# Token sums in sixteen steps among the weight parts, the next layer's memory norm inside the output product, and tanh for a reciprocal: a two-layer hybrid block on one core

## The chip, the cores and the metric

One core of a Trainium2 chip runs the whole kernel: two layers of a hybrid block for 1024 tokens of width 1024. Its engines are TensorE (PE), VectorE (DVE), ScalarE (ACT), GpSimd (POOL) and SyncE (SP); SP issues every DMA of this kernel, in order. The metric is the time of one execution on the device in microseconds, as the median of several runs.

## What is computed

Each layer normalizes the tokens, computes four branches (a gated MLP that mixes tokens in chunks, a sparse attention, an attention with a forget gate, an attention over a memory of 256 rows), multiplies each by a gate, adds them up, and projects the sum back onto the residual:

```python
def hybrid_layer(x, mem, ...):
    h = rms_norm(x, g_pre)
    parts = jnp.split(h @ w_in, IN_SPLITS, axis=-1)
    y_a = chunked_gmlp(a_u, a_v, ...) * jax.nn.silu(a_z)
    y_b = nsa_attention(b_q, ..., b_g, ...) * jax.nn.silu(b_z)
    y_c = forgetting_attention(c_q, c_k, c_v, c_f, c_fbias) * jax.nn.silu(c_z)
    y_m = memory_attention(m_q, mem, g_mem, w_mem_kv) * jax.nn.silu(m_z)
    ys = jnp.stack([y_a, y_b, y_c, y_m], axis=2)
    up = jnp.einsum('bsnw,nwd->bsnd', ys, w_br)
    gates = jax.nn.sigmoid(jnp.einsum('bsd,dne->bsne', h, w_gate))
    merged = jnp.einsum('bsnd,bsnd->bsd', gates, up)
    return x + rms_norm(merged @ w_o, g_post)
```

In `forgetting_attention` the gate enters as `log_sigmoid(f_logit + f_bias)`, summed over the tokens. In `memory_attention` the keys and values are `rms_norm(mem, g_mem) @ w_mem_kv`.

## The kernel before, in words

Every float32 matmul is done as three matmuls on operands split into a high and a low part. ACT copies the high part (L330) and DVE or POOL subtracts it from the operand to get the low one (`split`, L332). A block of weights is loaded by one DMA of 512 KB into one of two `wr` buffers, ACT copies `wh` (L227) and POOL subtracts `wl` (L229); for the names that begin with mk, mv, av and cv POOL does the first 512 columns and DVE the rest (L231).

A layer runs in this order. **The front** normalizes the memory rows and projects keys and values from them (`mem_kv`), then normalizes eight tiles of 128 tokens (`prenorm`); both transpose each tile on TensorE (L395). **The gates** follow. `proj_wide` (L300) multiplies a token half by a wide weight in four parts, 24 matmuls each; it runs for `av` on each half (each result goes through a GELU of two ACT and two DVE operations, L348 to L351, into `gv`) and for `cv` on each half. Between these products stands `token_sums`, a generator that prepares sums and differences of token quarters for a product with fewer multiplications (`quarter_mm`, L471). For each of four quarters POOL does four additions (L431), four operations on them (L432 to L435) and four split subtractions (L332: `t2l`, `t1l`, `t3l`, `t4l`), while ACT makes `t1h` to `t4h` after the last GELU. Nine `gate_pair`s of seven such products follow. Inside the first runs `forget`, the chain for the forget gate: ACT Abs (L561) and Exp (L564), DVE sums (L566, L567) and a reciprocal (L569), ACT `Ln` (L570), which needs another table in ACT, so a load of 1.28 us stands ahead of it and one behind. **The attention** stage computes the branches' heads; its outputs go to DRAM (`o`), are read back (`oo`, L1199), multiplied by a gate `z` (L340, L341, L1201) and stored (`y`, L1202). **The merge** reads a branch's `y` back as eight `yf` tiles (L1301), splits them into `yh` and `yl`, multiplies them by `u` weights (L251, L254, L255 on `yh`), and adds them up with gates `th` that are loaded (L1310) or computed. `out_proj` then multiplies the sum `mhh`, `mhl` by `w_o` for each token half (384 matmuls each), and the next layer's front begins.

The kernel is written in program order. A scheduler gives each engine and SP's DMA queue its own order, decided by the times that it reckons with. It also keeps the buffers of a pool in turn: the first write of a tile waits for the first write of the tile that stood before it in the same pool. `gate_out(1, "bz", 3)` is the last gate of the sparse attention: it reads what the last head stored and, in the kernel before, is called within branch 0 of the merge.

Of the kernel before, what the change touches and what calls it, by code (L numbers as in the profile page):

```python
# [19 lines left out]
F32 = mybir.dt.float32  # L20
# [193 lines left out]
class Net:  # L214
# [71 lines left out]

    def proj_wide(self, name, hi, lo, done, tail=False):


        v = "p (k c) -> p k c"  # L290
        ps = [self.pj() for _ in range(4)]
        for parts in ((0,), (1,), (2, 3)) if tail else ((0,), (1,), (2,), (3,)):
            w = [(x, [z.rearrange(v, c=512) for z in self.weight(f"{name}_{x}")]) for x in parts]
            for i in range(4):
                ts = slice(i * 128, i * 128 + 128)
                for x, (wh, wl) in w:
                    for k in range(2):
                        kk = 2 * x + k
                        for n, (a, b) in enumerate(((hi, wh), (hi, wl), (lo, wh))):
# [100 lines left out]
    def layer(self, l):  # L400
# [3 lines left out]
        nb = self.bufs  # L404
        with p("kf", 4) as self.pkk, p("vf", 3) as self.pvv, p("tf", 1) as self.ptp:
            self.front()
        with p("pp", nb["pp"]) as self.ppp:
# [9 lines left out]
    def token_sums(self):  # L417
# [8 lines left out]
        for k in range(4):  # L426
# [3 lines left out]
            for x, z in ((x11, b11), (x12, b12), (x22, b22), (x21, b21)):  # L430
                nc.tensor_add(x, f(z[0][:, k]), f(z[1][:, k]))  # L431
            nc.tensor_sub(x1, x12, x11)  # L432
            nc.tensor_sub(x22, x22, x12)
            nc.tensor_add(x11, x11, x22)
            nc.tensor_sub(x21, x21, x11)  # L435
            yield
            with self.tc.issue_after(self.last_act.ins):
                for n, x in (("t2", x11), ("t1", x1), ("t3", x22), ("t4", x21)):
                    self.split(t[n][0][:, k], t[n][1][:, k], x, pool=True)

# [113 lines left out]
    def forget(self):  # L554


        nc, fb, r = self.nc, self.fb[32:40], slice(32, 40)
        f, m, u = ([self.st(n)[r] for _ in range(2)] for n in ("ff", "fm", "fu"))
        x = [z[r] for z in self.fp]
        for c in range(2):  # L560
            nc.scalar.activation(f[c], x[c], AF.Abs, bias=fb)  # L561
            nc.vector.tensor_scalar(m[c], x[c], fb, 0.0, op0=OP.add, op1=OP.min)
        for c in range(2):
            nc.scalar.activation(f[c], f[c], AF.Exp, scale=-1.0)  # L564
        for c in range(2):
            nc.vector.tensor_scalar_add(u[c], f[c], 1.0)  # L566
            nc.vector.scalar_tensor_tensor(f[c], u[c], 1.0, f[c], op0=OP.subtract, op1=OP.subtract)  # L567
        for c in range(2):
            nc.vector.reciprocal(x[c], u[c])  # L569
            nc.scalar.activation(u[c], u[c], AF.Ln)  # L570
            nc.vector.tensor_mul(f[c], f[c], x[c])
# [105 lines left out]

    def fox_values(self, c):
        def done(i, ps):
            for x in range(2):  # L680
                self.value_tile(ps[:, x * 256:x * 256 + 256], c * 4 + i, x * 4)
        self.proj_wide("cv", self.hh[c], self.hl[c], done)

# [370 lines left out]

    def gmlp_v(self, c):

        def done(i, ps):
            t = self.st("gv")
            self.gelu2(t, ps, 512)
            self.nc.sync.dma_start(self.gvd[c * 4 + i], t)  # L1060
        self.proj_wide("av", self.hh[c], self.hl[c], done)

# [38 lines left out]

    def mem_kv(self):

        nc, a, l = self.nc, self.a, self.l
        mt = [[self.pkk.tile([128, 4, 256], R32, name="mt", tag="slot") for _ in range(2)] for _ in range(2)]
# [3 lines left out]
        with self.hot():  # L1109
            self.norm_t(a["mem"], a["g_mem"][l], 2, put)  # L1110
        m = lambda y, k: mt[y][k // 4][:, k % 4, :]
        for h in range(4):
# [104 lines left out]

    def front(self):
# [3 lines left out]
        self.mem_kv()  # L1222
        self.prenorm()
        self.early = True
        if self.l == 0:
            self.load("win", "anyc")

    def gates(self):
        sums = self.token_sums()
        self.turn2 = 0  # L1230
        next(sums)
        self.gmlp_v(0)
        next(sums)
        self.gmlp_w()
        self.gmlp_v(1)
        next(sums)
        self.fox_values(0)
        next(sums)
        self.fox_values(1)
        next(sums, None)  # L1240
        self.gmlp_sums()
# [28 lines left out]
    def merge(self):  # L1270
        nc, tc, a, l = self.nc, self.tc, self.a, self.l
        p = lambda n, b: tc.tile_pool(name=n, bufs=b, reuse_waits="tile")
        with p("acc", 1) as pacc, p("yh", 5) as self.pyh:
            self.acc = [pacc.tile([128, 8, 512], F32, name=f"acc{c}") for c in range(2)]
            for n in (0, 2, 3, 1):
                self.add_branch(n)
            gp = self.pyh.tile([128, 1024], F32, name="gp", tag="yh")
            nc.sync.dma_start(gp, a["g_post"][l].partition_broadcast(128))
            self.early = "banks"
            for c in range(2):  # L1280
                self.out_proj(c, gp)

    def add_branch(self, n):
        yy = [self.get_y(n, c) for c in range(2)]
        for cs in ((0, 1),) if n != 1 else ((0,), (1,)):
            for e in range(8):
                if n == 0 and e == 3:
                    self.gate_out(1, "bz", 3)
                wg = None if (n, e, 0) in self.ready else self.a_form(f"g{n}{e}")
# [158 lines left out]
```

## Time and profile before

| | |
|---|---|
| median of 3 runs (lowest to highest) | 3180.48 us (3177.91 to 3187.18) |
| profiled execution, its time | 3182.38 us |
| its span | 3180.3 us |
| TensorE busy (share) | 3056.4 us (96%) |
| DVE busy | 1876.5 us (59%) |
| ACT busy | 1485.2 us (47%) |
| POOL busy | 1450.7 us (46%) |

A busy share is an average over stages. In a timeline each row is an instruction with its start and duration in us, the engine, the line, the operation with its output and inputs, and in brackets the idle time of the engine before it with what released it. Lines are those of the kernel before.

### The profile page before, as it was taken

The numbers are of one execution on the slowest core, as the hardware profiler recorded it, in microseconds if no ns is written. First come the engines' busy times: TensorE is split into PE (matmuls) and PEld (weight loads), VectorE is DVE, ScalarE is ACT, GpSimd is POOL, SyncE is SP. The second block draws the span as 40 slices with busy tenths as digits, with TensorE's granted clock in tenths as the row PEclk, the third lists the DMA queues.
The fourth block names the chain that finished last, engine by engine and source line by source line (L and its number), as shares of the span: only waits on it lengthen the run. The fifth ranks groups of instructions, "written<-read, shape, count | busy, mean of one in ns | idle before, by whom it ended". The sixth has DMA issues, their size and how long they took to land.

```text
span 3180.3 us, 45150 instructions
## 1 busy us (share of the span) xinstructions
PE 3056.4 (96%) x15168; PEld 2554.8 (80%) x15168; DVE 1876.5 (59%) x4297; ACT 1485.2 (47%) x3309; POOL 1450.7 (46%) x1158
## 2 busy tenths in 40 slices
PE   7899999999999999999988999999999999999998
PEld 6678888887888888788776788788878888887887
DVE  6355447768666855336373554477686678653363
ACT  5333345556556555313353333455565555553232
POOL 6755445443232323258467444454432332332584
PEclk9999999999999999999999999999999999999999
DMA  6444486654334322456563444955542343234564
GB/s 219 127 133 130 149 252 170 181 178 128 101 106 146 110 88 93 149 172 196 187 194 122 136 133 146 256 171 173 186 133 88 112 142 107 87 96 159 175 195 146
DMA packets 251672, 475.15 MB, mean 149 GB/s; under 512 B 42512, under 2 KB 96784, under 8 KB 251440
## 3 DMA queue, kind: packets, MB, share of 16 engines
q1 hardware_dynamic: 251440, 472.26, 47.7%
q8 instruction: 120, 1.97, 0.3%
q14 instruction: 112, 0.92, 0.1%
HBM read 334.73 MB, written 137.43 MB: 148 GB/s over the span
## 4 chain that ended last, share of the span: by engine, by line
PE 81%; DMA 4%; POOL 4%; DVE 4%; issue 3%; ACT 3%; SPq 1%; DVEq 0%; POOLq 0%; ACTq 0%
PE pj L255 11%; PE pj L251 11%; PE pj L254 11%; PE s L471 6%; PE o L633 5%; PE s L300 5%; PE pt L621 5%; PE s L254 4%; PE pj L471 4%; PE s L255 4%; PE s L251 4%; PE pj L300 3%; PE s L589 3%; PE s L590 3%; POOL wl L229 2%
## 5 line engine op out<-in xcount | busy, mean ns | idle before, releaser
L229 POOL TENSOR_TENSOR wl<-wr,wh 128x1024 fp32r<-128x1024 f32 (+1 forms) x232 | 525.2, 2265 | 597.3 <-ACT wh L227 519.2
L255 PE MATMUL pj<-hh,wl 128*128 128x512 f32 x1648 | 652.1, 396 | 2.3 <-POOL wl L229 2.3
L251 PE MATMUL pj<-hh,wh 128*128 128x512 f32 x1648 | 651.2, 395 | 2.5 <-DVE z L341 1.9
L254 PE MATMUL pj<-hl,wh 128*128 128x512 f32 x1648 | 650.2, 395 | 0.0
L227 ACT ACTIVATE wh<-wr 128x1024 fp32r<-128x1024 f32 x232 | 245.7, 1059 | 361.5 <-DMA wr<-wt 90.6
L599 ACT ACTIVATE p<-p,nm 128x384 f32<-128x384 f32 (+3 forms) x512 | 306.8, 601 | 208.7 <-DVE nm L594 204.9
L332 DVE TENSOR_TENSOR pt<-pt,pt 128x512 fp32r<-128x512 f32 (+1 forms) x464 | 292.4, 635 | 145.7 <-ACT pt L330 144.3
L255 PEld LDWEIGHTS pj<-hh,wl 128*128 128x128 f32 x1648 | 310.5, 188 | 62.7 <-POOL wl L229 3.5
L251 PEld LDWEIGHTS pj<-hh,wh 128*128 128x128 f32 x1648 | 310.6, 188 | 60.8 <-DVE z L341 2.8
L330 ACT ACTIVATE pt<-pt 128x512 fp32r<-128x512 f32 (+1 forms) x464 | 252.3, 554 | 224.0 <-PE pt L621 164.6
L254 PEld LDWEIGHTS pj<-hl,wh 128*128 128x128 f32 x1648 | 310.3, 188 | 57.8
L633 PE MATMUL o<-pt,v 128*128 128x512 f32 (+1 forms) x864 | 245.6, 371 | 8.0 <-DVE pt L332 7.9
L642 POOL TENSOR_TENSOR yt<-yt 128x256 f32<-128x256 f32 x128 | 100.0, 781 | 293.8 <-ACT yt L641 234.1
L621 PE MATMUL pt<-ident,p 128*128 128x128 f32 x1488 | 231.3, 272 | 0.3 <-DVE pt L332 0.2
L621 PEld LDWEIGHTS pt<-ident,p 128*128 128x128 f32 x1488 | 185.1, 140 | 42.7 <-DVE pt L332 0.7
L251 PE MATMUL s<-yh,wh 128*128 128x512 f32 x512 | 200.2, 394 | 6.8 <-ACT yh L330 5.3
L589 PE MATMUL s<-kd,q 128*128 128x512 f32 (+2 forms) x512 | 187.5, 369 | 15.6 <-DVE nm L594 15.6
L254 PE MATMUL s<-yl,wh 128*128 128x512 f32 x512 | 200.9, 392 | 1.1 <-DVE yl L334 1.1
L255 PE MATMUL s<-yh,wl 128*128 128x512 f32 x512 | 200.2, 391 | 0.0
L590 PE MATMUL s<-kl,q 128*128 128x512 f32 (+2 forms) x512 | 175.7, 345 | 0.0
L633 PEld LDWEIGHTS o<-pt,v 128*128 128x128 f32 x864 | 147.9, 189 | 32.4 <-DVE pt L332 11.0
L664 DVE TENSOR_SCALAR p<-p,r,sg 128x384 f32<-128x384 f32 (+2 forms) x320 | 167.0, 577 | 1.7
(378 smaller groups left out, 6598.0 us busy)
## 6 DMA issues: line engine op xcount, KB each, us to landing
wr<-wt SPq DMA_DIRECT2D x250, 512.0 KB
th<-thd SPq DMA_DIRECT2D x124, 256.0 KB
thd<-gu SPq DMA_DIRECT2D x72, 256.0 KB
q<-rq SPq DMA_DIRECT2D x32, 512.0 KB
yf<-y SPq DMA_DIRECT2D x64, 256.0 KB
thd<-th SPq DMA_DIRECT2D x52, 256.0 KB
vd<-vs SPq DMA_DIRECT2D x48, 256.0 KB
v<-vd SPq DMA_DIRECT2D x24, 512.0 KB
```

What stands on the lines that cost most here:

```text
L229: nc.gpsimd.tensor_sub(lo[:, :n], raw[:, :n], hi.bitcast(F32)[:, :n])
L251: ins = nc.tensor.matmul(out, ah, bh, start=k == 0, stop=False)
L254: nc.tensor.matmul(out, ah, bl, start=False, stop=False)
L255: nc.tensor.matmul(out, al, bh, start=False, stop=k == n - 1)
L300: self.nc.tensor.matmul(ps[i], a[:, kk, ts], b[:, k], start=kk == n == 0, stop=kk == 7 and n == 2)
L332: (nc.gpsimd if pool else nc.vector).tensor_sub(lo, src, hi.bitcast(F32))
L471: nc.tensor.matmul(out, w[a][:, k], t[b][:, k], start=start and k == x == 0, stop=k == 3 and x == 2, skip_group_check=True)
L589: self.mark(nc.tensor.matmul(ps[:, :w], q[:, tq], kd[:, b0:b0 + w], start=True, stop=False), 1 + n / 128)
L590: nc.tensor.matmul(ps[:, :w], q[:, tq], kl[:, b0:b0 + w], start=False, stop=True)
L599: nc.scalar.activation(p[:, :n], p[:, :n], AF.Exp, bias=init, scale=-1.0, accum_out=l[:, x:x + 1])
L621: nc.tensor.transpose(pt[:, off + x * 128:off + x * 128 + 128], src, self.ident)
L633: nc.tensor.matmul(o[:, :, t0:t0 + m], it["v"], w[:, :, off:off + m], start=first, stop=last)
```

## The change

- `token_sums` yields sixteen times and not five, and `proj_wide` calls it (`among`) at each of its four weight parts, in `av` and `cv` on both halves. Each quarter is cut in four: the additions, the four operations, the splits of t2 and t1, the splits of t3 and t4. The subtractions of t3 and t4 move from POOL to DVE (`pool=False`).
- `mem_norm` is cut off from `mem_kv`. For layer 2 it is called between the two halves of the output product of layer 1, and `fresh`, `mem_kv` and `prenorm` of layer 2 directly behind the second half, within the merge and its pools.
- `gate_out(1, "bz", 3)` is called ahead of `add_branch(0)`.
- In `forget` the reciprocal of `1 + exp(-|x|)` becomes `0.5 + 0.5 tanh(|x| / 2)`: one ACT Tanh and one DVE operation for each half.

```diff
@@ proj_wide
             w = [(x, [z.rearrange(v, c=512) for z in self.weight(f"{name}_{x}")]) for x in parts]
+            among()
...
@@ token_sums
             for x, z in ((x11, b11), (x12, b12), (x22, b22), (x21, b21)):
                 nc.tensor_add(x, f(z[0][:, k]), f(z[1][:, k]))
+            yield
             nc.tensor_sub(x1, x12, x11)
             nc.tensor_sub(x22, x22, x12)
             nc.tensor_add(x11, x11, x22)
             nc.tensor_sub(x21, x21, x11)
             yield
-            with self.tc.issue_after(self.last_act.ins):
-                for n, x in (("t2", x11), ("t1", x1), ("t3", x22), ("t4", x21)):
-                    self.split(t[n][0][:, k], t[n][1][:, k], x, pool=True)
+            for pool, both in ((True, (("t2", x11), ("t1", x1))), (False, (("t3", x22), ("t4", x21)))):
+                with self.tc.issue_after(self.last_act.ins):
+                    for n, x in both:
+                        self.split(t[n][0][:, k], t[n][1][:, k], x, pool=pool)
+                yield
...
@@ forget
         for c in range(2):
+            nc.scalar.activation(x[c], f[c], AF.Tanh, scale=0.5)
             nc.scalar.activation(f[c], f[c], AF.Exp, scale=-1.0)
...
-            nc.vector.reciprocal(x[c], u[c])
+            nc.vector.tensor_scalar(x[c], x[c], 0.5, 0.5, op0=OP.mult, op1=OP.add)
...
@@ gates
         sums = self.token_sums()
         self.turn2 = 0
-        next(sums)
-        self.gmlp_v(0)
-        next(sums)
+        step = lambda: next(sums, None)
+        self.gmlp_v(0, step)
         self.gmlp_w()
-        self.gmlp_v(1)
-        next(sums)
-        self.fox_values(0)
-        next(sums)
-        self.fox_values(1)
-        next(sums, None)
+        self.gmlp_v(1, step)
+        self.fox_values(0, step)
+        self.fox_values(1, step)
...
@@ merge
-        with p("acc", 1) as pacc, p("yh", 5) as self.pyh:
-            self.acc = [pacc.tile([128, 8, 512], F32, name=f"acc{c}") for c in range(2)]
-            for n in (0, 2, 3, 1):
-                self.add_branch(n)
+        with p("yh", 5) as self.pyh:
+            with p("acc", 1) as pacc:
+                self.acc = [pacc.tile([128, 8, 512], F32, name=f"acc{c}") for c in range(2)]
+                self.gate_out(1, "bz", 3)
+                for n in (0, 2, 3, 1):
+                    self.add_branch(n)
...
-            for c in range(2):
-                self.out_proj(c, gp)
+            with p("kf", 4) as self.pkk, p("vf", 3) as self.pvv, p("tf", 1) as self.ptp:
+                self.out_proj(0, gp)
+                if l + 1 < self.depth:
+                    self.mem_norm(l + 1)
+                self.out_proj(1, gp)
+                if l + 1 < self.depth:
+                    self.l, self.xsrc = l + 1, self.x1
+                    self.fresh()
+                    self.mem_kv()
+                    self.prenorm()
...
@@ add_branch
-                if n == 0 and e == 3:
-                    self.gate_out(1, "bz", 3)
```

How the instructions stand then is shown at three places; the lines of the changed kernel are later by a few (L300 becomes L301, L332 L333, L395 L396, L431 L438).

POOL in the front, from the first quarter's last of four operations on (after: from its `t1l` on) (`w2r` holds the sums, `wl` a weight part). Before:

```order
L435 TENSOR_TENSOR w2r_761<-w2r_761,w2r_760 128x512
L332 TENSOR_TENSOR t2l_755<-w2r_760,t2h_754 128x512
L332 TENSOR_TENSOR t1l_753<-x1_762,t1h_752 128x512
L332 TENSOR_TENSOR t3l_757<-w2r_761,t3h_756 128x512
L431 TENSOR_TENSOR w2r_935<-hh0_500,hl0_502 128x512
L431 TENSOR_TENSOR w2r_935<-hh1_501,hl1_503 128x512
L332 TENSOR_TENSOR t4l_759<-w2r_761,t4h_758 128x512
L229 TENSOR_TENSOR wl_1061<-wr_1058,wh_1060 128x512
L229 TENSOR_TENSOR wl_1143<-wr_1140,wh_1142 128x512
L432 TENSOR_TENSOR x1_937<-w2r_935 128x512
L431 TENSOR_TENSOR w2r_936<-hh1_501,hl1_503 128x512
L431 TENSOR_TENSOR w2r_936<-hh0_500,hl0_502 128x512
```

After:

```order
L333 TENSOR_TENSOR t1l_764<-x1_773,t1h_763 128x512
L443 TENSOR_TENSOR w2r_772<-w2r_772,w2r_771 128x512
L333 TENSOR_TENSOR t2l_766<-w2r_771,t2h_765 128x512
L438 TENSOR_TENSOR w2r_961<-hh0_500,hl0_502 128x512
L438 TENSOR_TENSOR w2r_961<-hh1_501,hl1_503 128x512
L438 TENSOR_TENSOR w2r_962<-hh1_501,hl1_503 128x512
L438 TENSOR_TENSOR w2r_962<-hh0_500,hl0_502 128x512
L441 TENSOR_TENSOR w2r_962<-w2r_962,w2r_961 128x512
L1044 TENSOR_TENSOR wsr_935<-wsr_935,keep_937 128x512
L229 TENSOR_TENSOR wl_1065<-wr_1062,wh_1064 128x512
L229 TENSOR_TENSOR wl_1132<-wr_1129,wh_1131 128x512
L229 TENSOR_TENSOR wl_1170<-wr_1167,wh_1169 128x512
```

`t1l` stands ahead of the last operation, `t3l` and `t4l` are gone from POOL, and the weight parts stand behind all four additions of the next quarter and one of its operations. (On ACT `t1h` to `t4h` of this quarter stood behind the last of four GELUs; now they stand between the first and the third.)

SP's queue at the beginning of the first merge (`o` store, `oo` load, `yf` loads of branch 0, `th` gates). Before:

```order
L645 DMA o_116<-yt 64x256
L511 DMA thd<-th 128x512
L1301 DMA yf<-y_112 128x512 x8
L224 DMA wr<-wt 128x1024
L645 DMA o_116<-yt 64x256
L224 DMA wr<-wt 128x1024
L645 DMA o_116<-yt 64x256 x2
L1310 DMA th<-thd 128x512 x6
L1199 DMA oo<-o_116 128x512 x2
```

After:

```order
L1215 DMA oo<-o_116 128x512
L1218 DMA y_113<-z 128x512
L224 DMA wr<-wt 128x1024
L657 DMA o_116<-yt 64x256 x2
L1215 DMA oo<-o_116 128x512
L1316 DMA yf<-y_112 128x512 x5
L1218 DMA y_113<-z 128x512
L1316 DMA yf<-y_112 128x512 x3
L1325 DMA th<-thd 128x512 x12
```

The `yf` loads stood ahead of the last three `o` stores; now they stand behind them and behind the `oo` load that reads what these store.

TensorE at the end of layer 1's output product (`mhh`, `mhl`), where the second memory tile is transposed (`pt`) and multiplied (`mt`). Before:

```order
L300 MATMUL pj<-wh,mhh_14449 128x512
L300 MATMUL pj<-wl,mhh_14449 128x512
L300 MATMUL pj<-wh,mhl_14450 128x512
L395 MATMUL pt<-ident,x 128x128 x8
L251 MATMUL s<-mt,wh 128x256 x2
L251 MATMUL pj<-mt,wh 128x256
L254 MATMUL s<-mt,wh 128x256
```

After, the same transposes within the product:

```order
L301 MATMUL s<-wl,mhh_14451 128x512
L301 MATMUL s<-wh,mhl_14452 128x512
L301 MATMUL s<-wh,mhh_14451 128x512
L396 MATMUL pt<-ident,x 128x128 x8
L301 MATMUL s<-wl,mhh_14451 128x512
L301 MATMUL s<-wh,mhl_14452 128x512
L301 MATMUL s<-wh,mhh_14451 128x512
```

The transposes stood behind the last matmul of the product; now 137 of its 384 matmuls follow them.

## Rows read from the trace of the kernel before

**Rows 1.** Waits of TensorE: releaser; total us, times, longest us

```profile
PE pt L395 <- issue: 16.0, 4, 8.0
...
PE s L471 <- ACT gu L508: 14.0, 2, 7.0
...
PE s L300 <- POOL wl L229: 9.7, 8, 2.9
...
PE pj L300 <- DVE gv L351: 9.3, 2, 5.7
```

**Rows 2.** Timeline, PE, first front: start, us, operation, [idle <-releaser]

```profile
101.07 0.60 PE L300 MATMUL pj<-wl,hh 128*128 128x512 f32 x1 [3.33 <-POOL wl L229]
...
119.33 0.80 PE L300 MATMUL pj<-wh,hh 128*128 128x512 f32 x1 [3.62 <-DVE gv L351]
...
125.05 0.47 PE L300 MATMUL pj<-wl,hh 128*128 128x512 f32 x1
```

**Rows 3.** Timeline, POOL, 90 to 138 us

```profile
91.84 1.29 POOL L332 TENSOR_TENSOR t2l<-w2r,t2h 128x512 fp32r<-128x512 f32 x1 [6.34 <-ACT t2h L330]
...
99.75 2.50 POOL L229 TENSOR_TENSOR wl<-wr,wh 128x512 fp32r<-128x512 f32 x2
```

**Rows 4.** Timeline, ACT, first GELU of the second token half

```profile
116.57 0.60 ACT L348 ACTIVATE ge<-pj 128x512 f32<-128x512 f32 x1 [5.30 <-DMA ab<-bs]
```

**Rows 5.** Timeline, DVE, a subtraction beside POOL at 111 us

```profile
111.30 1.52 DVE L332 TENSOR_TENSOR wsl<-wsr,wsh 128x512 fp32r<-128x512 f32 x1
```

**Rows 6.** The weights' DVE subtraction: duration ns min/median/max

```profile
L231 DVE TENSOR_TENSOR wl<-wr,wh x48: 673/1390/1833, 12.4 to 1738.2; 128x512 fp32r<-128x512 f32 x48
```

**Rows 7.** Timeline, ACT, forget chain of the first layer

```profile
209.78 0.63 ACT L508 ACTIVATE gu<-gu 128x512 f32<-128x512 f32 x1
210.43 0.63 ACT L564 ACTIVATE ff<-ff 8x512 f32<-8x512 f32 x1
...
222.13 1.28 ACT L508 ACT_TABLE_LOAD   x1
```

**Rows 8.** Timeline, DVE, forget chain of the first layer

```profile
218.11 3.33 DVE L569 RECIPROCAL fp<-fu 8x512 f32<-8x512 f32 x1
```

**Rows 9.** Timeline, PE, 214 to 228 us

```profile
216.44 0.39 PE L471 MATMUL pj<-t4l,wh 128*128 128x512 f32 x1
216.66 0.39 PE L471 MATMUL pj<-t4h,wl 128*128 128x512 f32 x1
...
224.07 0.80 PE L471 MATMUL s<-t1h,wh 128*128 128x512 f32 x1 [7.02 <-ACT gu L508]
...
227.64 0.39 PE L471 MATMUL s<-t1h,wl 128*128 128x512 f32 x1
```

**Rows 10.** Timeline, PE, from the output product to the second layer

```profile
1603.04 2.19 PE L395 MATMUL pt<-ident,x 128*128 128x128 f32 x8 [7.96 <-issue]
...
1611.42 1.07 PE L395 MATMUL pt<-ident,x 128*128 128x128 f32 x8 [2.17 <-issue]
```

**Rows 11.** Window: PE, PEld, DVE, ACT, POOL busy us; clock; DMA share; GB/s

```profile
1600.00:1650.00 50.00, 42.55 (x291) 38.52 (x291) 39.67 (x69) 27.31 (x51) 32.65 (x29) 0.93 0.73 226
```

**Rows 12.** Chain of waits around the first merge: start us, us, what

```profile
1267.54 3.93 DMA o<-mo
...
1271.48 2.70 DMA oo<-o
...
1309.82 0.73 POOL yt L642
...
1316.01 4.86 DMA oo<-o
...
1320.95 0.61 ACT z L340
```

**Rows 13.** Timeline, PE, first matmul of the first merge

```profile
1311.69 0.50 PE L251 MATMUL s<-yh,wh 128*128 128x512 f32 x1 [2.64 <-ACT yh L330]
```

**Rows 14.** Timeline, SP, the loads of branch 0's inputs

```profile
1285.34 3.89 SPq L1301 DMA_DIRECT2D yf<-y  x8
```

More of the change, by code (lines that the diff above doesn't have):

```diff
@@ L285, in proj_t, with proj_wide @@
         return pt[:, :256]
-    def proj_wide(self, name, hi, lo, done, tail=False):
+    def proj_wide(self, name, hi, lo, done, tail=False, among=lambda: None):
         v = "p (k c) -> p k c"
@@ L404, in layer @@
         nb = self.bufs
-        with p("kf", 4) as self.pkk, p("vf", 3) as self.pvv, p("tf", 1) as self.ptp:
-            self.front()
+        if l == 0:
+            with p("kf", 4) as self.pkk, p("vf", 3) as self.pvv, p("tf", 1) as self.ptp:
+                self.fresh()
+                self.mem_norm(l)
+                self.mem_kv()
+                self.prenorm()
+                self.load("win", "anyc")
+        self.early = True
         with p("pp", nb["pp"]) as self.ppp:
@@ L676, in value_tile, with fox_values @@
         self.move(self.vd[h0:h0 + 4, :, i, :].rearrange("h p d -> p h d"), t)
-    def fox_values(self, c):
+    def fox_values(self, c, among):
         def done(i, ps):
@@ L681, in done @@
                 self.value_tile(ps[:, x * 256:x * 256 + 256], c * 4 + i, x * 4)
-        self.proj_wide("cv", self.hh[c], self.hl[c], done)
+        self.proj_wide("cv", self.hh[c], self.hl[c], done, among=among)
     def get(self, pool, src, name):
@@ L1053, in gmlp_sums, with gmlp_v @@
             nc.vector.scalar_tensor_tensor(ab[:, gs], ps[:, gs], lnb[:, g:g + 1], ab[:, gs], op0=OP.mult, op1=OP.add)
-    def gmlp_v(self, c):
+    def gmlp_v(self, c, among):
         def done(i, ps):
@@ L1060, in done @@
             self.nc.sync.dma_start(self.gvd[c * 4 + i], t)
-        self.proj_wide("av", self.hh[c], self.hl[c], done)
+        self.proj_wide("av", self.hh[c], self.hl[c], done, among=among)
     def gmlp_mix(self, i):
@@ L1099, in gmlp_u, with mem_norm @@
             nc.sync.dma_start(self.y[0][g, :, cs], u)
[L1102 to L1104 removed]
+    def mem_norm(self, l):
+        a = self.a
         mt = [[self.pkk.tile([128, 4, 256], R32, name="mt", tag="slot") for _ in range(2)] for _ in range(2)]
@@ L1110, in mem_kv @@
             self.norm_t(a["mem"], a["g_mem"][l], 2, put)
+        self.mt = mt
+    def mem_kv(self):
+        nc, mt = self.nc, self.mt
         m = lambda y, k: mt[y][k // 4][:, k % 4, :]
@@ L1216, in between, with fresh @@
         self.step += 1
-    def front(self):
+    def fresh(self):
         self.todo, self.step, self.marks, self.pace = [], 0, [], None
@@ L1221, in front @@
         self.ready = {}
[L1222 to L1226, printed above, removed]
     def gates(self):
@@ L1279, in merge @@
             self.early = "banks"
-            for c in range(2):
-                self.out_proj(c, gp)
+            with p("kf", 4) as self.pkk, p("vf", 3) as self.pvv, p("tf", 1) as self.ptp:
+                self.out_proj(0, gp)
[4 more added lines that the diff above has]
+                    self.l, self.xsrc = l + 1, self.x1
+                    self.fresh()
+                    self.mem_kv()
+                    self.prenorm()
     def add_branch(self, n):
```

## The prediction, made before the changed kernel ran

> **What bounds the kernel now.** I read the waits of TensorE first, then timelines around the longest of them, engine by engine, then the chain of waits. The profiled execution took 3182.4 us with a span of 3180.3, so 2.1 us lie outside; the median of the runs is 3180.5, 1.9 less. TensorE issues for nearly the whole span, so an edit pays only where TensorE stands. [rows 1] lists the places that the change touches. Four waits for memory or token rows to be transposed ("issue", 16.0 us) lie mostly between the layers. Two waits of 7.0 us for `gu` are one in each layer, while the forget chain runs. The waits for POOL's `wl` (9.7) and for `gv` (9.3) lie mostly in the fronts, where the token sums share POOL with the weights. Each long wait also costs clock: after the 7.02 us wait the next eight matmuls take 3.57 us from start to start [rows 9], 0.45 each, where two before it are 0.22 apart: half the rate, the lower of the clock's two levels. That is 1.8 us more for one wait.
>
> **Token sums in sixteen steps.** Before, after ACT has split a quarter's sums, POOL does `t2l`, `t1l`, `t3l`, two additions of the next quarter and `t4l` in one row, from 91.84 us, and the weight part that TensorE needs next stands behind them at 99.75 [rows 3]. TensorE waits 3.33 us for it at 101.07 [rows 2], then 2.9 for a later part [rows 1]. Later the second token half's first GELU starts at 116.57, released by a DMA of `ab` [rows 4], so its banks come free late and TensorE waits 3.62 at 119.33 [rows 2]. The 13 steps from there to 125.05 take 5.72 us where 13 at 0.22 take 2.9: 2.8 us of clock. With 1.8 for the clock after the first wait, the front of the first layer loses 3.33 + 2.9 + 3.62 + 2.8 + 1.8 = 14.4 us.
>
> In the new order `t3l` and `t4l` go to DVE, and ACT makes `t1h` to `t4h` between the first half's GELUs and not after the last, so POOL need not stand the 6.34 us ahead of 91.84 [rows 3]. It ended its work before at 85.5 and would now have `t1l` in front of that work's last operation, from 84.2. From there to the weight part stand nine operations, 9 x 1.29 = 11.6, and the part's own 1.25 (half of the 2.50 at 99.75): done at about 97.1, with some blocking 97.5, when TensorE asks for it, and 3.5 before 101.0. The second half's first GELU takes its buffer after POOL's `x1` and not after the `ab` load. Ahead of `x1` stand two more weight parts; the third's load can start when the first one's buffer is free, at 97.5, so I estimate that part at 104.5, `x1` and the GELU at 106, ten ahead of 116.57. What is new: the third and fourth weight parts come one POOL operation late each, 1.29 x 2 = 2.6. I take 14.4 - 2.6 = 12 us. The second layer has the same pattern, its `gv` wait longer, 5.7 [rows 1], its `wl` waits shorter; I take 12 again. Sum **-24**. From below, only the wait at 101.07 goes (3.33 + 1.8 = 5 a layer); from above, all of it (14 to 16 a layer, the waits under 1 us included): -10 to -32. I stay nearer the upper end because the GELU's releaser is an order of buffers, visible in [rows 4], and not work.
>
> The eight DVE subtractions of a layer lie beside POOL work. The nearest row, DVE's half of the weights' subtraction, takes from 0.67 to 1.83 us, median 1.39 [rows 6], and `wsl` at 111.30, while POOL works, took 1.52 [rows 5]. So I cost each at 1.4; in the GELU chain DVE waits for ACT about as long between two steps, so 0.7 of each is covered and the rest, 0.7 x 2 before the bank is free, lies inside my margin.
>
> The Trainium skill, "SBUF — State Buffer", section "Who interferes with whom", says that a VectorE instruction with two SBUF inputs contends with a GpSimd instruction that reads SBUF, one of them blocking for all of the other. The spread of rows 6 agrees. By that rule the eight subtractions can give back up to their own time on POOL, 8 x 0.67 = 5.4 us a layer; that is the third rival below.
>
> **Tanh for the reciprocal.** The two DVE reciprocals of a chain take 3.33 us each [rows 8], four in the kernel. They stand ahead of the `Ln` that ACT must do before it loads its table back (1.28 us at 222.13 [rows 7]) and reads the bank `gu` that TensorE waits for until 224.07 [rows 9]. The added Tanh costs 0.63 twice, as the Exp of the same shape [rows 7], one of them beside DVE's work; it needs no table load, since Tanh at 209.78 and Exp at 210.43 stand back to back [rows 7]. The DVE operation in the reciprocal's place needs the Tanh alone and stands ahead of the chain to `Ln`. Taking out 2 x 3.33 and adding 0.63 moves ACT's `gu` from 223.4 to 217.4 and TensorE's start from 224.07 to 218.0; its last matmul before ends at 217.05. So 1.0 of the 7.02 stays: 6.0 gained, and 1.8 of clock, **8 a layer, -16** for both. From below 5 a layer (a `wh` that ACT does first is late), from above 8.8: -10 to -17.6.
>
> **Memory norm of layer 2 inside the output product.** Between the layers TensorE stands 7.96 us before the second memory tile's transposes and 2.17 before the first token tile's [rows 10]. In the new order these transposes stand after 247 and 283 of the 384 matmuls of the second half's product, and the memory projections follow the product at once: 10.1 us go. I take **-10**. What comes next is the rate at which weights and token tiles arrive: 226 GB/s with the DMA engines 0.73 busy [rows 11]. From below 0 (TensorE, in order, stands at a transpose whose row comes late, as it did between the layers, or the same 10 us reappear before the token products), from above 16 (the lower clock there goes too). I take the middle, what [rows 10] show.
>
> **The b branch's last gate ahead of branch 0.** This is the new cost. Before, the eight loads of branch 0's inputs (`yf`) are issued at 1285.34 [rows 14], long before TensorE's first use at 1311.69 [rows 13]. In the new order they stand on SP's in-order queue behind the last `o` store and the `oo` load that waits for that store's landing, and the first `yf` also waits for ACT's `z` from that `oo`. No matmul is queued on TensorE that doesn't need `yh` from `yf`. POOL's last product starts at 1309.82, a second follows, and the store is issued at about 1311.8. From there: a store to landing 3.93, an `oo` load 2.70 (before, among other loads, it took 4.86), `z` 0.61 [rows 12], a `yf` load as long as the `oo`, 2.70, and ACT's split 0.6: 1311.8 + 10.5 = 1322.3, against 1311.69. I take **+11 a layer, +22**; the clock loss is there before as well. With 4.86 for both loads it is 15. From below 0: nothing waits, if the buffer that `yf` takes is another than I read. Range 0 to +30.
>
> **Sum.** -24 - 16 - 10 + 22 = -28: 3182.4 - 28 = 3154 for a profiled execution, 3180.5 - 28 = 3152 against the median.
>
> **Rivals.**
> 1. *No wait at the merge.* All else as above: 3180.5 - 50 = 3130. For it: SP has little else to do there. Against: the order on the queue is fixed. 0.15.
> 2. *The boundary gives nothing*, the time returning before the token products because DMA is 0.73 busy: 3162. 0.12.
> 3. *The fronts give back most.* Between the third and the fourth weight part of the second half ten POOL operations stand in a row, 10 x 1.29 = 12.9 us, more if DVE's subtractions block them (1.39 against 0.67 [rows 6]). If the fronts gain 4 a layer, 8 in place of 24: 3168. For it: POOL is already the releaser [rows 1]. By the rule of the Trainium skill named above this would be the likelier case; the trace shows blocking but not its share on the path. 0.18.
> 4. *Slower: the queue's fence starves the merge twice.* Eight `yf` loads are 2 MB, 9.3 us at 226 GB/s [rows 11]; if they land together the first matmul comes at about 1329, 17 later than now. The store of `z` stands among them, waiting for DVE and POOL, so the other token half stands again for about 10, and two more losses of clock are 3.6: 31 a layer. 3180.5 - 50 + 62 = 3192. It decides from 30 a layer (25 is even). Against: `oo` alone took 2.70 at this place [rows 12]. 0.05.
>
> **How the numbers follow.** Forecast 0.50 (3142 to 3163 by its own bounds), the rivals 0.15, 0.12, 0.18 and 0.05. What a measurement of this kernel can tell from no change is about 0.3%, 9.5 us. Rivals 1 and 2 are faster, as is most of 3 (it ends within 0.3% if the merge costs 15 a layer too); so faster 0.86, within 0.3% 0.08, slower 0.06. The range reaches from rival 1's to a little beyond rival 3's, **3128 to 3172**.
>
> **What would show it.** TensorE's wait for `gu` under 1.5 us in both layers; the `wl` waits around 100 to 115 us gone and `gv` no longer a releaser of TensorE; no wait for transposes of 8 us between the layers; and one wait for `yh` of some 11 to 15 us at each merge, ACT's split being released by a DMA of `yf`. It would be wrong if POOL's `wl` stays a releaser with ten us or more in the fronts, or if that merge wait is missing or twice as long.

## The result

The changed kernel takes 3153.7 us (median of 4 runs, 3151.5 to 3157.7), the kernel before 3179.2 in the same runs: ratio 0.991, interval 0.9895 to 0.9925, faster by 25 us between the medians. 3152 was predicted. The profiled execution of the changed kernel took 3157.7 with this head of its page (span, then busy us, share of the span and number of instructions of each engine):

```profile
span 3155.9 us, 45143 instructions
PE 3047.0 (97%) x15168; PEld 2548.8 (81%) x15168; DVE 1884.3 (60%) x4313; ACT 1487.9 (47%) x3313; POOL 1439.2 (46%) x1142
```

TensorE is busy for 97% of the span in place of 96. Its waits, in the view of [rows 1] (releaser; total us, times, longest):

```profile
PE s L251 <- ACT yh L331: 24.7, 2, 12.6
...
PE pt L396 <- issue: 10.0, 4, 4.3
...
PE s L301 <- POOL wl L229: 6.6, 4, 3.0
...
PE pj L481 <- DVE gu L513: 3.6, 2, 1.8
PE pj L301 <- DVE gv L352: 3.2, 2, 2.2
PE pj L301 <- POOL wl L229: 2.8, 3, 1.4
...
PE s L481 <- ACT gu L518: 1.3, 2, 0.7
```

Two rows of the kernel before belong beside them that [rows 1] does not have:

```profile
PE pj L300 <- POOL wl L229: 6.5, 3, 3.3
PE s L251 <- ACT yh L330: 5.3, 2, 2.6
```

The two waits of 7.0 us for ACT's `gu` are 1.3 us together, and the longest wait for transposes released by `issue` is 4.3, at the kernel's start, in place of 8.0. Those for `wl` at these products are 9.4 in place of 16.2, those for `gv` 3.2 (with a short one on `s`, 3.8) in place of 9.3. A wait that was 5.3 us in all before, for `yh`, is 24.7. And one is new: `gu` on DVE, 1.8 us in each layer.

Lining up the starts of TensorE's first and last matmul of each stage in both traces gives the account by stage (us, changed minus before, profiled execution against profiled execution):

| stage | layer 1 | layer 2 |
|---|---|---|
| start to the first wide product | -1.9 | (boundary) |
| wide products, with the token sums | -10.3 | -7.8 |
| on to the first hundred matmuls of the gate pairs, with the forget chain | -7.2 | -8.1 |
| rest of the gate pairs | +2.1 | +1.2 |
| attention, to the merge's first matmul | +7.6 | +12.2 |
| merge | -0.9 | +0.4 |
| output product | +1.3 | 0.0 |
| boundary, to layer 2's first wide product | -13.0 | |
| sum | -22.3 | -2.1 |

In all -24.4, the difference of the spans. The first line is no part of the change: five kernels below that change nothing there start their wide products 0.5 to 2.9 us earlier than the profiled execution of before, too. The attention line holds scatter as well: in two kernels below that change nothing in that stage (tanh alone; `t3` and `t4` on DVE in five steps) it is +3.3 and +4.0 in layer 1, -0.8 and -1.0 in layer 2. Counted from the 128th last `o` product of the heads to the merge's first matmul, those two agree with the kernel before to 0.1 us, and the changed kernel is 8.8 and 9.6 us longer.

### The profile page after: what moved, and what is told of

The parts are those of the page before. It is cut to its first block, busy times and chain, and to the rows that moved or that the text cites. A ratio compares the mean times of both kernels' runs of the same rounds, so it can differ in the third digit from the quotient of the medians.

```text
span 3155.9 us, 45143 instructions
## 1 busy us (share of the span) xinstructions
PE 3047.0 (97%) x15168; PEld 2548.8 (81%) x15168; DVE 1884.3 (60%) x4313; ACT 1487.9 (47%) x3313; POOL 1439.2 (46%) x1142
## 4 chain that ended last, share of the span: by engine, by line
PE 82%; DVE 5%; DMA 4%; POOL 3%; issue 2%; ACT 2%; SPq 1%; DVEq 0%; POOLq 0%; ACTq 0%
PE pj L251 11%; PE pj L254 11%; PE pj L255 11%; PE s L481 5%; PE s L301 5%; PE s L254 5%; PE o L645 5%; PE s L251 5%; PE s L255 5%; PE pt L633 5%; PE pj L481 4%; PE pj L301 4%; PE s L601 3%; PE s L602 3%; DVE p L674 1%
## 5 line engine op out<-in xcount | busy, mean ns | idle before, releaser
L333 DVE TENSOR_TENSOR pt<-pt,pt 128x512 fp32r<-128x512 f32 (+1 forms) x464 | 291.9, 635 | 134.8 <-ACT pt L331 133.4
L251 PE MATMUL s<-yh,wh 128*128 128x512 f32 x512 | 201.1, 396 | 24.7 <-ACT yh L331 24.7
```

The costliest lines, as they stand in the source:

```text
L251: ins = nc.tensor.matmul(out, ah, bh, start=k == 0, stop=False)
L333: (nc.gpsimd if pool else nc.vector).tensor_sub(lo, src, hi.bitcast(F32))
```

## The experiments

Each ran beside the kernel before, in four groups in which that takes 3180.8 (gate inside, inputs first, sums alone, tanh alone), 3182.2 (gate alone, norm alone, all on POOL, `t3` and `t4` in five steps), 3184.5 (two pools, norm first, gate later) and 3182.7 us (the scan). Across groups the ratios compare better than the times. "Stage" numbers below are from lining up traces as above.

### The gate back inside branch 0

```diff
-                self.gate_out(1, "bz", 3)
                 for n in (0, 2, 3, 1):
                     self.add_branch(n)
...
             for e in range(8):
+                if n == 0 and e == 3:
+                    self.gate_out(1, "bz", 3)
```

> The changed kernel with the b branch's last gate called again inside branch 0, as before; the other three edits stay. My theory: the merge's new wait for yh comes from the yf loads standing behind the last o store and the oo load on SP's queue, so it goes back to about 2.6 us a layer and the time falls by some 19 to 21 us from 3153.7, to 3133 or so, ratio to the kernel before about 0.985. Rival (the wait comes from the acc and yh pools having changed places, or from the earlier end of the attention stage): the wait for yh stays at 12 us a layer and the time stays within 4 us of 3154.

Measured: 3131.8 us, ratio 0.984 (0.982 to 0.9859), 22 us better than the changed kernel. The wait for `yh` is 0.5 us at both merges. Two rows of TensorE's waits:

```profile
PE pt L396 <- issue: 10.6, 5, 3.6
...
PE s L251 <- DVE acc L1333: 2.8, 2, 1.5
```

What is left are waits for transposes, 1.8 us a layer for `gu` behind the forget chain, and 1.4 a layer for `acc`. The gate's new place is what cost time, 11 us a layer. This version beats both kernels.

### Branch 0's inputs written ahead of the gate

```diff
+                yy = [self.get_y(0, c) for c in range(2)]
                 self.gate_out(1, "bz", 3)
                 for n in (0, 2, 3, 1):
-                    self.add_branch(n)
+                    self.add_branch(n, yy if n == 0 else None)
```

> The changed kernel with the gate still ahead of branch 0, but the loads and splits of branch 0's inputs written ahead of the gate; on SP's queue the eight yf loads then stand ahead of the last stores again. My theory (order of loads on the queue, not the gate's place): the wait for yh is under 4 us a layer and the time 3132 to 3137, like the run with the gate inside. Rival (the gate's own chain of store, load, ACT and POOL work delays the merge wherever the loads stand): 3145 to 3154, with a wait of 6 us or more for yh, s or acc at the merge's start.

Measured: 3138.5 us, ratio 0.9867 (0.9849 to 0.9885); 15 of the 22 us come back, less than my theory said and more than the rival did. The wait for `yh` is 0.5 us, but another stands 15 us behind it. DVE at the first merge:

```profile
1302.68 1.30 DVE L1333 SCALAR_TENSOR_TENSOR acc<-th,s 128x512 f32<-128x512 f32 x2 [2.14 <-DMA th<-thd]
```

and on TensorE there:

```profile
1288.30 0.51 PE L251 MATMUL s<-yh,wh 128*128 128x512 f32 x1 [0.48 <-ACT yh L331]
...
1303.42 0.79 PE L251 MATMUL s<-yh,wh 128*128 128x512 f32 x1 [6.17 <-DVE acc L1333]
```

The gates `th` of branch 0 stand on SP's queue behind the `oo` load and a store, as the `yf` loads did, so DVE's `acc` waits for a `th` load and TensorE 6.2 us for `acc`. So the order of loads on SP makes the wait, but of all loads that stand behind that store and that `oo` load (the fence, in what follows), not of `yf` alone.

### The token sums alone

The kernel before, with the edits of `proj_wide`, `token_sums`, `gates` and the two callers:

```diff
+            for pool, both in ((True, (("t2", x11), ("t1", x1))), (False, (("t3", x22), ("t4", x21)))):
...
+                yield
...
+        step = lambda: next(sums, None)
+        self.gmlp_v(0, step)
...
```

> The kernel before with the token sums in sixteen steps (t3 and t4 subtracted on DVE) as the only edit. My theory: the two fronts gain 12 and 9 us as in the changed kernel's trace and nothing takes it back, so 3179 - 21 = 3158, ratio 0.993. Rival (what the fronts gain is partly given back where the attention's units wait for other engines): 3165 to 3172, ratio 0.996 to 0.998.

Measured: 3156.5 us, ratio 0.9922 (0.9904 to 0.9939). Stages: the wide products of layer 1 -10.4, of layer 2 -10.5, and nothing of it comes back behind them (0.0 and -1.2 in the gate pairs behind the first hundred matmuls). My theory holds.

### Tanh alone

The kernel before, with the edit of `forget`:

```diff
+            nc.scalar.activation(x[c], f[c], AF.Tanh, scale=0.5)
...
-            nc.vector.reciprocal(x[c], u[c])
+            nc.vector.tensor_scalar(x[c], x[c], 0.5, 0.5, op0=OP.mult, op1=OP.add)
```

> The kernel before with tanh for the forget chain's reciprocal as the only edit. My theory: the waits of 7.0 us for gu fall to about 1 us, 7 us a layer with the clock, but a wait of up to 1.8 us for the next gu on DVE appears behind it, so 11 to 14 us in all: 3165 to 3168, ratio 0.9955 to 0.9965. Rival (in the changed kernel the gain came from the front's earlier end and not from tanh): under 5 us, 3175 or more.

Measured: 3170.0 us, ratio 0.996 (0.9946 to 0.9974), 11 us. Stages: -7.2 to the chain's end in both layers, then +2.9 and +1.0 in the gate pairs. Tanh does it, and a part comes back, as my theory said.

### The gate ahead of branch 0 alone

The kernel before, with this alone:

```diff
+            self.gate_out(1, "bz", 3)
             for n in (0, 2, 3, 1):
                 self.add_branch(n)
...
-                if n == 0 and e == 3:
-                    self.gate_out(1, "bz", 3)
```

> The kernel before with the b branch's last gate called ahead of branch 0 as the only edit. My theory (SP's queue puts the yf loads behind the last store and the oo load): a wait for yh of 12 us at both merges and 3181 + 19 to 22 = 3200 to 3203, ratio 1.006 to 1.007. Rival (the cost arises only together with the pools that the changed kernel opens in the merge): no change, 3178 to 3184, and the run with the gate inside gained by something else.

Measured: 3201.2 us, ratio 1.0063 (1.0046 to 1.008): 19 us slower. Its wait:

```profile
PE s L251 <- ACT yh L330: 24.6, 2, 12.3
```

That is 12.3 us a layer against the 2.64 of [rows 13], 19.3 more in all. The cost does not need the other edits.

### The memory norm alone

The kernel before, with `mem_norm`, `mem_kv`, `fresh` and `merge` of the changed one, the gate still within branch 0:

```diff
-            for c in range(2):
-                self.out_proj(c, gp)
+                self.out_proj(0, gp)
+                if l + 1 < self.depth:
+                    self.mem_norm(l + 1)
+                self.out_proj(1, gp)
...
```

> The kernel before with layer 2's memory norm inside the output product, its memory projections directly behind it, and the gate still inside branch 0; neither the token sums nor tanh. My theory: the two waits of 8.0 and 2.2 us between the layers go, the output product is some 1 to 2 us longer by the inserted transposes, and 3181 - 12 = 3169, ratio 0.996; with the parts measured so far (24 for the sums, 11 for tanh, 49 for all three) it should be 14 at most. Rival (DMA-bound boundary, the time returns before the token products): under 5 us, 3176 or more.

Measured: 3161.2 us, ratio 0.9932 (0.9917 to 0.9947): 21 us, 9 more than I expected. The boundary's part is what I said (output product +2.4, then -13.4). What I had not seen is that both attention stages end 3.4 us earlier, measured from the last heads' first outputs to the merge's first matmul. These are 6.8 of the 9 us; the rest I cannot place. That the time returns before the token products did not come true.

### Two pools in another order

```diff
-        with p("acc", 1) as pacc, p("yh", 5) as self.pyh:
+        with p("yh", 5) as self.pyh, p("acc", 1) as pacc:
```

> The kernel before with one line changed: the pool of the merge's inputs (yh) is opened ahead of the accumulators' pool (acc), as in the changed kernel. In the runs with the norm inside the product the attention stage ended 3.4 us a layer earlier than by its edits. My theory: that comes from the swap, because the inputs then lie where buffers were freed earlier, so the first matmul of the merge stands ahead of the last head's last two; the merge begins 3 to 3.5 us a layer earlier and 3182 - 7 = 3175, ratio 0.998. Rival (scatter of the attention stage between kernels): 3179 to 3185 and the wait of 2.6 us for yh stays.

Measured: 3182.5 us, ratio 0.9993 (0.9983 to 1.0003). The time says the rival, the trace says why it does: the attention stages do end 3.4 us earlier in both layers, TensorE's first matmul of the merge standing ahead of the last head's last two with no wait of 2.6 us, as its first row there shows:

```profile
1306.48 0.50 PE L251 MATMUL s<-yh,wh 128*128 128x512 f32 x1 [0.49 <-ACT yh L330]
```

But with the pools so, both memory tiles of layer 2 are transposed behind the output product, and the first one's row comes late there. The waits of TensorE for `x` (the first of the two is at the kernel's start, as before):

```profile
PE pt L395 <- DVE x L392: 24.3, 2, 15.7
```

The longest is 15.7 us, where before the two waits at this place were 8.0 and 2.2 (released by `issue`). So the swap gives 3.4 us a layer and by itself loses 5.3 at the boundary. In the changed kernel the norm's new place takes the 15.7 us away, and the 3.4 are hidden: the gate's fence ends the attention stage later than the inputs could be ready. So the fence costs 22 us there (against the run with the gate inside), 19 alone.

### All subtractions on POOL

The token sums alone, with this edit:

```diff
-            for pool, both in ((True, (("t2", x11), ("t1", x1))), (False, (("t3", x22), ("t4", x21)))):
+            for pool, both in ((True, (("t2", x11), ("t1", x1))), (True, (("t3", x22), ("t4", x21)))):
```

> The kernel before with the token sums in sixteen steps but all four subtractions on POOL. My theory: both halves of the edit are needed; with two more operations of 1.3 us per quarter POOL has 12 a quarter plus the weight parts, about as long as TensorE's work for them, so it keeps a part of the waits for wl and the gain is 10 to 17 us in place of 24: 3164 to 3171. Rival A (the finer steps alone do it, the moved subtractions are only relief): as with both, 3155 to 3159. Rival B (by the rule on VectorE and GpSimd sharing reads, subtractions on DVE cost POOL what they save, so POOL alone does as well or better): 3150 to 3157.

Measured: 3160.3 us, ratio 0.9931 (0.9916 to 0.9946), 3 to 4 us behind the token sums alone by ratio and time; the intervals overlap, so the total does not tell the two apart. Stages: wide products of layer 1 -11.0, as good as with DVE; of layer 2 -3.6 in place of -10.5. There TensorE's waits are 9.8 us in place of 5.2, the longest for DVE's half of a weight part:

```profile
1702.65 0.80 PE L301 MATMUL s<-wl,hh 128*128 128x512 f32 x1 [4.25 <-DVE wl L231]
```

My 10 to 17 us were too few; the finer steps alone do most (nearest to rival A). That DVE's help counts in layer 2 is what this one pair of traces shows.

### Only t3 and t4 moved to DVE, in five steps

```diff
-                for n, x in (("t2", x11), ("t1", x1), ("t3", x22), ("t4", x21)):
-                    self.split(t[n][0][:, k], t[n][1][:, k], x, pool=True)
+                for n, x in (("t2", x11), ("t1", x1), ("t3", x22), ("t4", x21)):
+                    self.split(t[n][0][:, k], t[n][1][:, k], x, pool=n in ("t1", "t2"))
```

> The kernel before with its five steps kept and only the subtractions of t3 and t4 moved to DVE. My theory: in POOL's order the two additions that were behind come forward into the places left free, so the weight part at 99.75 us is as late as before; the wait of 3.3 us stays and the gain is 0 to 8 us, 3173 to 3181. Rival (the relief of POOL is what gains): 15 us or more, 3166 or less.

Measured: 3182.1 us, ratio 1.0001 (0.9991 to 1.001). No gain; the waits for `wl` rise and only those for `gv` fall:

```profile
PE s L300 <- POOL wl L229: 13.6, 6, 4.4
...
PE pj L300 <- POOL wl L229: 8.2, 3, 4.2
...
PE pj L300 <- DVE gv L351: 4.5, 2, 3.6
```

Eight subtractions fewer on POOL in each layer are worth nothing while its order keeps the weight part at the row's end: all four additions of the next quarter now stand ahead of it, and TensorE's wait there, 3.33 us in [rows 2], is 4.2.

### The norm ahead of both halves

On the version with the gate inside branch 0:

```diff
-                self.out_proj(0, gp)
                 if l + 1 < self.depth:
                     self.mem_norm(l + 1)
+                self.out_proj(0, gp)
                 self.out_proj(1, gp)
```

> The run with the gate inside, and the memory norm of layer 2 ahead of both halves of the output product in place of between them. My theory: of the waits that are left between the layers (3.6 us at the first memory tile, 3.3 behind the product) the first stays, since the tile's transposes stand as early in the product as before and now two tiles come one behind the other there; 3130 to 3137, within 0.2% of 3132. Rival (the place of the norm still costs): 3 us or more better, 3129 or less.

Measured: 3131.2 us, ratio 0.9833 (0.9818 to 0.9849): the same as with the norm between the halves (0.984), as expected, and the wait at the first memory tile stays (3.5 us).

### The gate later in branch 0

Again on the version with the gate inside:

```diff
-                if n == 0 and e == 3:
+                if n == 0 and e == 6:
```

> The run with the gate inside, the gate called at e == 6 of branch 0 in place of e == 3. My theory: with the oo load well landed by then, the waits of 1.5 us for acc at the merge's start (2.8 in all) go and nothing else changes: 3128 to 3131. Rival (the gate's two groups of matmuls move later and its product is needed by branch 1's loads, or the wait for acc has another cause): 3132 or more.

Measured: 3145.8 us, ratio 0.9876 (0.9859 to 0.9893), 14 us worse by time and 11 by ratio. The waits for `acc` did not go (3.6 us in all, 2.8 with the call at e == 3). The rival's time holds, by a road that I had not seen. With the call at e == 3 the order takes the gate's 48 matmuls forward into the last heads; at e == 6 they stay in the merge (96 of this kind stand there in place of 48), which is 12 to 14 us longer than with e == 3, while the attention stage is only 5 to 8 shorter, since TensorE there now waits for the heads:

```profile
1272.36 0.77 PE L641 MATMUL o<-pt,vcm 128*128 128x256 f32 x2 [4.13 <-DVE pt L333]
```

### The forget chain's scan behind the first gate pair

On the version with the norm first; `end` is called in the second gate pair:

```diff
-        for c in range(2):
-            nc.vector.tensor_sub(f[c], u[c], f[c])
...
+        def end():
+            with self.tc.issue_after(self.last_gu.ins):
+                for c in range(2):
+                    nc.vector.tensor_sub(f[c], u[c], f[c])
...
+        return end
```

> The run with the gate inside and the norm first, and the forget chain's last part (two differences and the scan for each half, on DVE) written so that it is issued behind the first gate pair's last sum. With tanh TensorE waits 1.8 us a layer for that sum on DVE, and about 2 of the 7.2 us gained at the chain go again. My theory: the scan stood ahead of the sum on DVE's queue, so the wait of 1.8 goes in both layers and the stretch from the chain to the last gate pair is 1 to 2 us shorter a layer, 3128 to 3130. Rival (the later scan delays the next gate pair's first sums by as much): the stretch stays within 0.7 us, 3130 to 3133.

Measured: 3134.9 us, ratio 0.9853 (0.9836 to 0.9871), 4 us behind the run it changes by time and 6 by ratio, with intervals that overlap. The wait of 1.8 us is gone and a longer one comes behind it:

```profile
216.32 0.50 PE L481 MATMUL s<-hh,wh 128*128 128x512 f32 x1 [2.26 <-DVE gu L499]
```

The gate pairs after the chain are 2.4 us longer in layer 1 and 1.7 in layer 2 than without the edit. So neither range holds; the rival's cause does, and costs more than it allowed. The scan must be done somewhere, and this place on DVE's queue is not free either.

## Why the prediction was right

No term fell: each wait that was to go went or shrank, and the one that was to come came. That the time came out within 2 us of the forecast is partly luck. The medians differ by 25.5 us where 28 were forecast, and by stages the four edits give -22.5, the rest being the start. The sizes were off by 2 to 5 us each: the sums and tanh gave 10 less than forecast, the norm and the gate 4.4 better, and these errors cancel in part.

Of the signs that were named, those for tanh, the boundary and the merge came as said, the sign for the fronts only in part. Waits for `wl` of 0.3 to 1.7 us stay between 96 and 107 us, `gv` still releases TensorE, and POOL's `wl` stays a releaser with 9.4 us at these products, near the ten that would have spoken against the term. The runs with the sums alone and with its two halves are what shows that term.

**Token sums, -24 predicted; -19 by stages** (-10.3 in layer 1, -7.8 and, behind the wide products, -0.9 in layer 2); alone they gave 24. The steps of the first front came as worked out. POOL in the changed kernel:

```profile
85.04 1.30 POOL L333 TENSOR_TENSOR t2l<-w2r,t2h 128x512 fp32r<-128x512 f32 x1
...
94.24 2.98 POOL L229 TENSOR_TENSOR wl<-wr,wh 128x512 fp32r<-128x512 f32 x2
...
103.49 1.74 POOL L440 TENSOR_TENSOR x<-w2r 128x512 f32<-128x512 f32 x1
105.19 1.72 POOL L229 TENSOR_TENSOR wl<-wr,wh 128x512 fp32r<-128x512 f32 x1
...
108.12 1.72 POOL L333 TENSOR_TENSOR t1l<-x,t1h 128x512 fp32r<-128x512 f32 x1
```

`t2l` starts at 85.04, where before POOL stood 6.34 us and began it at 91.84 [rows 3]; the weight part starts at 94.24 (the row holds two parts), and TensorE has it at 96.03. The forecast was 97.5, and this front starts 1.9 us earlier by the profiled execution alone, so 95.6. The GELU then waits for POOL's `x`:

```profile
105.27 0.60 ACT L349 ACTIVATE ge<-pj 128x512 f32<-128x512 f32 x1 [1.80 <-POOL x L440]
```

At 105.27, where 106 - 1.9 was estimated, against 116.57 [rows 4]. TensorE in this stretch has no wait over 2 us, where [rows 2] has 3.33 and 3.62:

```profile
96.03 0.50 PE L301 MATMUL pj<-wl,hh 128*128 128x512 f32 x1 [0.26 <-POOL wl L229]
...
102.24 0.49 PE L301 MATMUL s<-wh,hh 128*128 128x512 f32 x1 [0.22 <-ACT wh L227]
103.59 0.50 PE L301 MATMUL s<-wl,hh 128*128 128x512 f32 x1 [0.86 <-POOL wl L229]
...
106.97 0.50 PE L301 MATMUL s<-wl,hh 128*128 128x512 f32 x1 [1.72 <-POOL wl L229]
...
109.36 0.66 PE L301 MATMUL pj<-wh,hh 128*128 128x512 f32 x1 [0.98 <-DVE gv L352]
```

The waits here sum to 4.0 us against the 2.6 that I left, 2.8 of them for `wl` and 1.0 for `gv`. Layer 2 is where the term was too large, since two waits stay there that "the same pattern, 12 again" did not see:

```profile
1670.19 0.50 PE L301 MATMUL pj<-wh,hh 128*128 128x512 f32 x1 [2.23 <-DVE gv L352]
...
1689.37 0.50 PE L301 MATMUL s<-wl,hh 128*128 128x512 f32 x1 [3.02 <-POOL wl L229]
```

With the sums alone the second is there too (2.96), the first is not, and the layer gained 10.5; so the 2.7 us that are missing go with the wait for `gv`, and why it comes with the other edits is not shown. The subtractions cost what I took for them, 1.4:

```profile
106.93 1.77 DVE L333 TENSOR_TENSOR t3l<-w2r,t3h 128x512 fp32r<-128x512 f32 x1 [0.35 <-ACT t3h L331]
...
L333 DVE TENSOR_TENSOR t3l<-w2r,t3h x8: 693/1416/1780, 80.3 to 1707.6; 128x512 fp32r<-128x512 f32 x8
```

They take from 0.69 to 1.78 us, so the blocking of the Trainium skill's "SBUF — State Buffer", section "Who interferes with whom", is in this trace too. POOL's `t1l` at 108.12 starts while DVE's `t3l` of 106.93 still runs and takes 1.72, where `t2l` at 85.04 takes 1.30; `wl` at 105.19 also takes 1.72, beside DVE's half of a weight part. What it would have made of the time, the third rival, did not come: the wide products gained 10.3 and 7.8 us and not 4 each, and the sums with all four subtractions on POOL are no better than with two on DVE.

**Tanh, -16 predicted; -11 by stages.** TensorE's wait is what I said, 1.0 predicted, 0.67 measured, and the matmuls behind it start 0.23 apart, so no clock is lost:

```profile
205.53 0.50 PE L481 MATMUL s<-t1h,wh 128*128 128x512 f32 x1 [0.67 <-ACT gu L518]
...
213.09 0.50 PE L481 MATMUL pj<-t3h,wh 128*128 128x512 f32 x1 [1.83 <-DVE gu L513]
```

The step to the chain's end gained 7.2 a layer (8 predicted). What the working left out stands in the second row: 1.83 us for `gu` from DVE. On DVE's queue ahead of it:

```profile
209.21 1.60 DVE L587 TENSOR_TENSOR_SCAN fm<-ff 8x512 f32<-8x512 f32 x1
210.84 1.59 DVE L462 TENSOR_TENSOR ws<-w2r 128x512 f32<-128x512 f32 x1
212.36 0.68 DVE L513 TENSOR_TENSOR gu<-gu,pj 128x512 f32<-128x512 f32 x1
```

With the reciprocals gone the chain's scan (`fm`, 1.60 us) stands ahead of L513, a sum that TensorE waits for. Before, the same sum (L503 there) stood ahead of the scan:

```profile
224.72 0.68 DVE L503 TENSOR_TENSOR gu<-gu,pj 128x512 f32<-128x512 f32 x1
...
228.92 1.21 DVE L575 TENSOR_TENSOR_SCAN fm<-ff 8x512 f32<-8x512 f32 x1
```

The prediction asked what is late next on ACT and TensorE, and not on DVE.

**Norm in the output product, -10 predicted; -11.7 by stages** (-13.0 at the boundary, +1.3 in the product). The wait for the first memory tile stays in the product:

```profile
1508.73 0.84 PE L396 MATMUL pt<-ident,x 128*128 128x128 f32 x4 [2.83 <-issue]
```

and behind it, where [rows 10] had 7.96 and 2.17, there are

```profile
1599.05 0.63 PE L396 MATMUL pt<-ident,x 128*128 128x128 f32 x4 [1.55 <-issue]
...
1604.68 0.66 PE L396 MATMUL pt<-ident,x 128*128 128x128 f32 x4 [1.70 <-DVE hl L333]
```

so 10.1 us of waits became 3.3, at other tiles, and the granted clock, 0.92 of full speed in the 44 us behind the product before, is 1.00 in the 31 us of the changed kernel. The size of the term is partly luck: the prediction let all 10.1 us of waits go and left the clock to its upper bound; 6.9 went, and the clock makes up most of the rest (0.08 of 44 us are 3.5, an estimate). (The 384 matmuls that the prediction counts for the product's second half are those of both halves, 192 each.) The second rival, a bound by DMA, does not hold: DMA is 0.78 busy there (0.73 in [rows 11]) and TensorE gains all the same.

**The gate ahead of branch 0, +22 predicted; +19.3 by stages.** The chain of waits at the first merge:

```profile
1291.92 0.73 POOL yt L656
...
1292.67 1.92 DMA o<-yt
...
1294.64 2.69 DMA oo<-o
...
1297.36 0.61 ACT z L341
...
1297.98 3.33 DMA yf<-y
...
1301.34 0.64 ACT yh L331
...
1302.02 0.79 PE s L251
```

Store, `oo`, `z`, `yf`, `yh`: the steps and their order are those of the forecast. The store lands in 1.92 us where I took 3.93 from [rows 12], `oo` takes 2.69 (2.70 taken), `yf` 3.33 (2.70 taken): from the store to the matmul 9.4 us in place of 10.5, with errors both ways. The wait of TensorE is 12.1 us in layer 1 and 12.6 in layer 2, against 2.64 [rows 13]. The fourth rival, a fence that starves the merge twice, did not come: one wait only, and the merge itself is no longer. The first rival, no wait, is out.

**What the prediction missed.** The change's new order of pools lets the merge begin 3.4 us a layer earlier, and the gate's move hides that. It is in no term, since only the fence's own cost was asked for, and not what else the pools' order does. It does not show in the total; against the run with the gate inside the fence costs the 22 us of the forecast, against the kernel before 19, and only the second is what was forecast.

**What stays open.** The three gains measured alone multiply to 0.9922 x 0.996 x 0.9932 = 0.9815, and together (the run with the gate inside) they are 0.984, 8 us less. Their intervals, of about 0.0016 each, leave room for that; whether the edits overlap by some microseconds isn't settled. By stages 2.7 of it lie in layer 2's wide products, which gain 10.5 with the sums alone and 7.7 together.

## What to carry to other kernels

A load that is off the path only because it was issued early is on the path as soon as anything that waits is put ahead of it on the same queue: before an edit moves a call, list what its DMAs will stand in front of. Finer steps, placed where the consumer has work, can gain more than work moved to another engine: here the same POOL work in sixteen steps gained 22 us, and fewer operations in five steps none. When a wait on one engine goes, work on another can come to stand ahead of what is needed next: look at each queue of the shortened chain for what moves up.

## What the runs showed of the hardware

The clock's loss hardly grew with the wait. Behind the 12.1 us wait of the changed kernel the first twelve matmuls of the merge take 5.59 us from start to start (1302.02 to 1307.61), most of them 0.43 apart, then 0.23; behind the 2.64 us wait of the kernel before twelve take 4.94 (1311.69 [rows 13] to 1316.63). The thirteenth matmul in both:

```profile
1307.61 0.40 PE L254 MATMUL s<-yl,wh 128*128 128x512 f32 x1
...
1316.63 0.39 PE L254 MATMUL s<-yl,wh 128*128 128x512 f32 x1
```

In layer 2 they take 5.59 and 4.68. So a wait that was 9.5 to 10 us longer cost 0.6 to 0.9 us more clock. A 64 KB store landed in 1.92 us in one trace at the merge, where the `mo` store that I took for it needed 3.93 in the other (128 KB, the DMA engines 0.80 busy in that time and 0.15 in the first); the `oo` load of 256 KB took 2.69 and 2.70 with the DMA engines 0.34 and 0.33 busy and 4.86 behind six `th` loads with 0.67.
